# One core, a decoder layer: more expert tiles split ahead, gathers moved earlier, two score maps interleaved, gate loads reordered

## The chip, the core and the metric

The kernel runs on one NeuronCore of one Trainium2 chip. The metric is the device time of one execution in microseconds (us). Before the change the median of three runs is 1810.1 us (1809.93 to 1811.16). The engines are TensorE (PE for its matmuls, PEld for its weight loads), VectorE (DVE), ScalarE (ACT), GpSimd (POOL) and SyncE (SP, which only issues transfers). ACT and POOL also issue transfers, in their own order with their other work.

## The reference

One decoder layer on 512 tokens of width 1024, in two sub-layers, each `x <- LN_affine(ALPHA*x + gate*sublayer(h))` with `h = LN(x)*(1+scale)+shift`; shifts, scales and gates come from `silu(c) @ w_ada`.

Sub-layer 1 is a differential attention (8 heads, two score maps of 64 features per head, causal) beside a chunkwise matrix memory (4 heads), merged by sigmoid gates and projected. Sub-layer 2 is a retrieval over 128 x 128 = 16384 single-neuron experts:

```
q = (ht @ w_q).reshape(T, 8, 2, 64)            # 8 heads, two half keys
s = einsum('thpd,pnd->thpn', q, sub_keys)      # 2 maps of 128 scores per head
sv, si = top_k(s, 16)                          # of each map
cv, ci = top_k(sv0[:, None] + sv1[None], 16)   # of the 256 sums
g = softmax(cv);  eidx = i1 * 128 + i2
act = gelu(einsum('cd,chkd->chk', h, u_tab[eidx]))
out = einsum('chk,chkd->cd', g * act, v_tab[eidx])
```

Each token so uses 8 x 16 = 128 rows of `u_tab` and of `v_tab`.

## The kernel before

**Number format.** Every product of two f32 operands is three f16 matmuls (high x high, high x low, low x high). A weight tile of 128x1024 is loaded as f32 (`raw`, three buffers), split by ACT (the high part) and DVE (the low part) into `w2` (eight buffers), and used by PE. `presplit(n)` (L186) does the same ahead of time for tiles that are needed later: SP loads the tile into one of two halves of a buffer named `pre`, ACT and DVE split it, and ACT's queue writes both parts (512 KB) to `us` in DRAM. `load_p` (L199) then loads them with one transfer and no splitting; a tile that isn't in `us` goes through `raw`. `NP` tiles are pre-split: the 8 `q` tiles of layer two, then the `u` tiles in order.

**Layer one.** PE's program is written by hand (class `Ordered`): each matmul is chained to the one before it. Blocks of work that PE can do at any time (projections) stand in a queue `F`, and `F.run(ns)` puts so many nanoseconds of them between the steps of the attention. A step (`at_s`, L446) makes two score maps of one head and 128 queries: for each map three matmuls with 64 contraction rows (map 0 uses rows 0 to 63, map 1 rows 64 to 127), and one full-height matmul that adds the causal mask. DVE takes each map's row maximum, ACT the exponentials, DVE joins the maps. There are 32 steps; one `presplit(1)` stands in each of the first 27. In the merge that follows, eight rounds `j` each queue up to four blocks of 24 matmuls, and `presplit(PRE_M)` with `PRE_M` = 2 stands at the end of each round before `F.drain()`; one more follows the loop.

**Layer two, routing.** Token tile 0 (128 tokens) is served sparsely: `dots` gathers 128 rows of `u_tab` per token by 128 indirect transfers (POOL issues, 512 KB each) and DVE multiplies each with `h` and adds it up (L873); later 128 gathers of `v_tab` rows follow, with a multiply-add each (`accg`, L1235). Token tiles 1 to 3 are served densely: all 128 `u` tiles against 384 tokens, a gate mask multiplied in, and all 128 `v` tiles. `route(t)` (L940) finds the experts of tile t: `scores` (L925) makes one map of four heads, 12 matmuls of 64 rows and 128 columns, into one PSUM bank that ACT copies out to `sb`; DVE finds the top 16 of each of 16 maps and then of 8 sums; tiles 1 to 3 then build one-hot matrices on DVE and multiply them on PE to gate masks that go to DRAM (`gd`). `F` now holds the first 72 `u` tiles, whose results go to DRAM (`actd`). `some(dotg, 1)` lets DVE do one gather dot: after each of the four groups of maps and in each of the nine one-hot rounds, 13 per tile, 39 in all. Their gathers have two buffers there.

**Layer two, dense part.** The 32 rounds of `order` each take four `u` and `v` tiles. For 14 rounds the `u` products are made on the spot (`u_round`, 96 matmuls of 384 columns); for the last 18 they are loaded back from `actd` ("held" rounds). `gate(n)` multiplies the mask `gblk`, loaded by `gate_load`. `v_round` does 72 matmuls of 512 columns into six PSUM banks. The rest of the sparse work (89 dots, 128 multiply-adds) is let in by credits: 1.8 per `u` tile from the second `u_round` on, 1 per `v` tile, and what is left in the last round. `finish` normalises a token tile. The stage begins with a load of `h2r` (tile 0's `h`) from DRAM, `gate_row(gt2, g2r)` (eight transposes on PE, two copies on ACT) and six mask loads, ahead of the first `u_round`.

**What sets the order.** A scheduler orders each engine's program by the data dependencies and by where things stand in the code; on the chip each engine and each queue works its list in order, and waits at the first entry that isn't ready.

## Time and profile before

| | before |
|---|---|
| median of 3 runs | 1810.1 us |
| the profiled execution: time / span | 1810.87 / 1808.8 us |
| PE, DVE, ACT, POOL busy | 94%, 79%, 45%, 25% of the span |
| mean granted TensorE clock | 0.982 of full speed |
| DMA | 484.89 MB, mean 268 GB/s |

The span runs from the first to the last instruction; the execution's own time is 2.1 us longer. Reading in order of time: to 92 us start-up and first projections, 92 to 345 the attention steps, to 420 the matrix memory, to 572 the merge, to 640 the output projection and the start of layer two, 640 to 1036 the routing of tiles 0 to 3, 1036 to 1465 the dense rounds with `u` work, to 1795 the held rounds and the last one, then the end on DVE. A busy share is an average: a PE that shows 10 of 10 in a window has no idle time there, and there its own work sets the pace.

### The profile page before, as it was taken

How to read it: one execution, taken by the hardware profiler on the slowest of the kernel's cores; microseconds unless marked ns; L12 is line 12 of the kernel's file. 1: busy time of each engine (PE TensorE's matmuls, PEld its weight loads, DVE VectorE, ACT ScalarE, POOL GpSimd, SP SyncE). 2: the span in 40 equal slices, each digit the busy share in tenths (PEclk: the TensorE clock that was granted, in tenths of full speed). 3: DMA queues.
4: the chain of work that ended last, by engine and by line, in shares of the span. 5: the costliest groups of instructions: out<-in, count | busy, mean ns of one | idle time of the engine just before them, and what ended most of it. 6: DMA issues, size and time to landing. Idle time of an engine off the chain costs nothing.

```text
span 1808.8 us, 26501 instructions
## 1 busy us (share of the span) xinstructions
PE 1704.3 (94%) x9937; PEld 915.9 (51%) x9937; DVE 1423.5 (79%) x2702; ACT 813.1 (45%) x1279; POOL 452.6 (25%) x296
## 2 busy tenths in 40 slices
PE   5999999989999989999998899999999998988996
PEld 2444455445444666766655555555555543433443
DVE  7787877697666798969989658888878777577796
ACT  4556666564343433636737543333333333232332
POOL 0000000000000100110210135554556445345551
PEclk9999999989999999999999999999999999999999
DMA  8554754347776536895976999999999999988982
GB/s 337 170 191 168 248 195 142 105 157 273 273 277 231 210 114 222 285 306 193 305 258 222 334 347 357 389 349 343 341 376 331 333 336 321 342 287 320 331 325 80
DMA packets 223104, 484.89 MB, mean 268 GB/s; under 512 B 16000, under 2 KB 114560, under 8 KB 222976
## 3 DMA queue, kind: packets, MB, share of 16 engines
q1 hardware_dynamic: 124912, 286.06, 46.0%
q0 software_dynamic: 36864, 134.23, 20.2%
q10 hardware_dynamic: 61200, 62.92, 10.1%
q8 instruction: 77, 1.26, 0.3%
q14 instruction: 51, 0.42, 0.1%
HBM read 418.14 MB, written 65.01 MB: 267 GB/s over the span
## 4 chain that ended last, share of the span: by engine, by line
PE 58%; DVE 16%; DMA 9%; issue 8%; POOL 4%; ACT 3%; ACTq 1%; SPq 0%; DVEq 0%; POOLq 0%
PE mm L101 32%; PE s L101 15%; PE tr L101 6%; POOL gat L865 3%; PE o L101 3%; DVE w L169 2%; DMA gat<-in_v_dram,ev 2%; DMA gd<-gstage 1%; PE tr L104 1%; DMA vraw<-in_v_dram 1%; DMA raw<-in_u_dram 1%; DVE accg L1235 1%; DVE gat L873 1%; ACTq L914 1%; DMA at<-actd 1%
## 5 line engine op out<-in xcount | busy, mean ns | idle before, releaser
L101 PEld LDWEIGHTS <-w 128*128 128x128 f16 x7176 | 690.5, 99 | 669.3 <-issue 30.1
L101 PE MATMUL mm<-h2T,w 128*128 128x384 f16 (+2 forms) x3288 | 558.0, 327 | 12.0 <-ACT ast L857 7.4
L101 PE MATMUL s<-w,w 128*128 128x512 f16 x1152 | 275.4, 384 | 25.7 <-DVE w L169 25.7
L865 POOL DMA_INDIRECT gat<-in_v_dram,ev x128 | 240.3, 1878 | 227.6 <-DVE accg L1235 210.9
L865 POOL DMA_INDIRECT gat<-in_urows_dram,eu x128 | 179.5, 1403 | 447.6 <-DVE gat L873 352.0
L169 DVE SCALAR_TENSOR_TENSOR w<-raw,w 128x1024 f16<-128x1024 f32 x180 | 218.8, 1219 | 73.6 <-ACT w L168 73.1
L168 ACT ACTIVATE w<-vraw 128x1024 f16<-128x1024 f32 x128 | 134.9, 1055 | 284.2 <-DMA vraw<-in_v_dram 158.4
L168 ACT ACTIVATE w<-raw 128x1024 f16<-128x1024 f32 x180 | 188.2, 1053 | 85.6 <-DMA raw<-in_u_dram 34.1
L101 PE MATMUL mm<-h1T,w 128*128 128x512 f16 x960 | 219.0, 379 | 1.8 <-DVE cva L624 1.8
L101 PE MATMUL tr<-w,w 128*128 128x512 f16 x768 | 187.0, 380 | 0.0
L169 DVE SCALAR_TENSOR_TENSOR w<-vraw,w 128x1024 f16<-128x1024 f32 x128 | 155.2, 1217 | 20.2 <-ACT w L168 20.0
L1235 DVE SCALAR_TENSOR_TENSOR accg<-gat,wg,accg 128x1024 f32<-128x1024 f32 x127 | 162.3, 1278 | 10.1 <-DMA gat<-in_v_dram,ev 9.5
L1283 DVE TENSOR_TENSOR at<-at,gblk 128x1536 f32<-128x1536 f32 x32 | 56.2, 1755 | 81.1 <-DMA at<-actd 70.7
L873 DVE SCALAR_TENSOR_TENSOR gat<-gat,rows 128x1024 f32<-128x1024 f32 x89 | 107.9, 1220 | 12.5 <-DMA gat<-in_urows_dram,eu 12.4
L101 PE MATMUL mm<-w,h1T 128*128 128x512 f16 x456 | 107.7, 382 | 3.6 <-ACT h1T L168 1.8
L101 PE MATMUL o<-w,w 128*128 128x512 f16 x384 | 105.4, 385 | 0.0
L101 PEld LDWEIGHTS <-h1T 128*128 128x128 f16 x672 | 58.3, 98 | 66.0 <-issue 2.5
L165 POOL TENSOR_TENSOR ss<-ss,mhalf 128x4 f32<-128x4 f32 x8 | 8.1, 1017 | 314.7 <-DVE ss L510 284.2
L857 ACT ACTIVATE at<-mm 128x384 f32<-128x384 f32 x56 | 27.4, 489 | 129.8 <-PE mm L101 126.3
L1050 ACT ACTIVATE gstage<-tr 128x512 f32<-128x512 f32 x96 | 56.5, 598 | 55.3 <-PE tr L101 37.9
L169 DVE SCALAR_TENSOR_TENSOR pre<-pre 128x1024 f16<-128x1024 f32 x44 | 53.8, 1222 | 31.4 <-ACT pre L168 30.6
L101 PEld LDWEIGHTS <-onehot 128*128 128x128 f16 x768 | 64.0, 148 | 19.6 <-issue 9.5
(460 smaller groups left out, 1837.0 us busy)
## 6 DMA issues: line engine op xcount, KB each, us to landing
vraw<-in_v_dram SPq DMA_DIRECT2D x128, 512.0 KB, 7.5
raw<-in_u_dram SPq DMA_DIRECT2D x92, 512.0 KB, 6.5
raw<-in_wz_dram SPq DMA_DIRECT2D x64, 512.0 KB, 4.3
w<-us SPq DMA_DIRECT2D x52, 512.0 KB, 4.5
wad<-in_w_ada_dram SPq DMA_DIRECT2D x48, 512.0 KB, 5.1
gd<-gstage ACTq DMA_DIRECT2D x24, 1024.0 KB, 9.3
gblk<-gd SPq DMA_DIRECT2D x64, 384.0 KB, 9.9
us<-pre ACTq DMA_DIRECT2D x44, 512.0 KB, 4.1
```

Source lines behind the costliest of these rows:

```text
L101: self._link(self.tc.nc.tensor.matmul(*a, **k))
L104: self._link(self.tc.nc.tensor.transpose(*a, **k))
L165: G.tensor_tensor(o, i, mhalf[:, :i.shape[1]], op=ALU.pow)
L168: A.activation(hi, src, AF.Copy, scale=scale)
L169: V.scalar_tensor_tensor(lo, src, scale, hi, op0=ALU.mult, op1=ALU.subtract)
L857: A.activation(dst, ps[:, :TD], AF.Gelu, scale=RU)
L865: P.before(G.indirect_dma_start(out=g_, out_offset=None, in_=table, in_offset=bass.IndirectOffsetOnAxis(ap=e[:, k:k + 1], axis=0)))
L873: V.scalar_tensor_tensor(g_, g_, 1.0, ring["h2r"], op0=ALU.mult, op1=ALU.mult, accum_out=wg[:, k:k + 1])
L914: nc.scalar.dma_start(actd[k], a.rearrange("p a b -> p (a b)"))
L1050: A.activation(st[:, :, 4 * q4:4 * q4 + 4], ps.rearrange("p t i -> p i t"), AF.Copy, scale=1.0 / S_G)
L1235: V.scalar_tensor_tensor(accg, g_, wg[:, k:k + 1], accg, op0=ALU.mult, op1=ALU.add)
L1283: V.tensor_tensor(av, av, GB[q_ // 2][:, :, e].rearrange("p g e t -> p e g t"), op=ALU.mult)
```

## The change

- `NP` 44 to 64: `u` tiles 36 to 55 are pre-split too. 13 of them stand in the attention steps (a second `presplit` in every other one of the first 27 steps, after the transposes), so 40 there; the merge has 3 instead of 2 per round, 24 in all, each now followed by `F.run(5500)` rather than together; none is left after the loop.
- `some(dotg, 1)` stands after every second map search and every second search in the sums: 8 + 4 + 9 = 21 per tile, 63 in all. 65 dots are left for the dense part.
- `at_s` and `scores` make both maps in turn: a matmul of map 0, the same of map 1, and so on; in `at_s` both masks follow, then both maxima. `scores(t, hq)` fills two PSUM banks; for tiles 2 and 3 both are made at the end of the routing of the tile before, where one was.
- `gate_row(gt2)` and a 512 KB store of its result go to the start of layer two; the dense part loads `h2r` and `g2r` together (1 MB) from DRAM. The first four mask loads and this load come after the first `u_round`'s loads in the code, two more after them.

The core of the diff:

```
-NP = 44
+NP = 64
+PRE_H = 0.5
-PRE_M = 2
+PRE_M = 3
+FILL_P = 5500
...
-                for m in range(2):
-                    r = slice(64 * m, 64 * m + 64)
-                    sm = ps_s()
-                    sms.append(sm)
-                    P.matmul(sm[:, :n], q[r, 0, qs], k[r, 0, :n], start=True, stop=False)
-                    P.matmul(sm[:, :n], q[r, 0, qs], k[r, 1, :n], start=False, stop=False)
-                    P.matmul(sm[:, :n], q[r, 1, qs], k[r, 0, :n], start=False, stop=False)
+                sms = [ps_s(), ps_s()]
+                for a, b in ((0, 0), (0, 1), (1, 0)):
+                    for m in range(2):
+                        r = slice(64 * m, 64 * m + 64)
+                        P.matmul(sms[m][:, :n], q[r, a, qs], k[r, b, :n],
+                                 start=a + b == 0, stop=False)
+                for sm in sms:
                     P.matmul(sm[:, qs], identb, negm, start=False, stop=True)
+                for m, sm in enumerate(sms):
                     V.tensor_reduce(nm[:, m:m + 1], sm[:, :n], axis=AX.X, op=ALU.max, negate=True)
...
+                if n < PRE_N:
+                    presplit(int((n + 1) * PRE_H) - int(n * PRE_H))
...
-                presplit(PRE_M)
+                for _ in range(PRE_M):
+                    presplit(1)
+                    F.run(FILL_P)
                 F.drain()
...
-                    if n < 3:
-                        scores(t, *banks[n + 1])
+                    if n == 1:
+                        scores(t, 1)
...
-                    if t > 0:
-                        some(dotg, DOT_S)
+                        if t > 0 and k % 2 == 1:
+                            some(dotg, DOT_S)
...
+                    if t > 0 and h % 2 == 1:
+                        some(dotg, DOT_S)
...
-        nc.sync.dma_start(h2r, h2d)
-        gate_row(gt2, g2r)
...
+                    if n == 0 and i == 3:
+                        for k in range(4):
+                            gate_load(0, k)
+                        nc.sync.dma_start(rows[:, 0:2], h2d)
...
-            for k in range(6):
-                gate_load(k // 4 * 2, k % 4)
             u_round(0, SP_0)
+            for k in range(2):
+                gate_load(2, k)
```

PE's program in an attention step, before, from the third matmul of map 0 on (`s_803` and `s_809` are the PSUM banks of the two maps, `identb` the weights of the mask matmul):

```order
L101 LDWEIGHTS q_624
L101 MATMUL s_803<-k_657,q_624 128x128
L101 LDWEIGHTS identb_82
L101 MATMUL s_803<-negm_88,identb_82 128x128
L101 LDWEIGHTS q_624
L101 MATMUL s_809<-k_657,q_624 128x128
L101 LDWEIGHTS q_624
L101 MATMUL s_809<-k_657,q_624 128x128
```

The same step after; `s_803` and `s_804` are the two maps:

```order
L103 LDWEIGHTS q_624
L103 MATMUL s_803<-k_657,q_624 128x128
L103 LDWEIGHTS q_624
L103 MATMUL s_804<-k_657,q_624 128x128
L103 LDWEIGHTS identb_82
L103 MATMUL s_803<-negm_88,identb_82 128x128
L103 LDWEIGHTS identb_82
L103 MATMUL s_804<-negm_88,identb_82 128x128
```

Map 0's mask stood between the maps; now the six narrow matmuls alternate and both masks stand behind them. The number of instructions is the same.

SP's queue at the start of the dense part, before (`raw` are `u` tiles, `gblk` mask loads, the first row of `h2d` the load of `h2r`):

```order
L173 DMA raw<-in_u_dram 128x1024 x37
L1187 DMA rows_10955<-h2d 128x1024
L173 DMA raw<-in_u_dram 128x1024 x2
L1259 DMA gblk<-gd 128x6x128 x3
L173 DMA raw<-in_u_dram 128x1024 x2
L1259 DMA gblk<-gd 128x6x128 x3
L173 DMA raw<-in_u_dram 128x1024 x2
L1259 DMA gblk<-gd 128x6x128
```

The same place after:

```order
L175 DMA raw<-in_u_dram 128x1024 x23
L1312 DMA vraw<-in_v_dram 128x1024
L1272 DMA gblk<-gd 128x6x128 x4
L1293 DMA rows_11039<-h2d 128x2048
L1272 DMA gblk<-gd 128x6x128 x3
L1312 DMA vraw<-in_v_dram 128x1024
```

The `u` tiles up to the tenth of the dense part now stand ahead of every mask load, and the load from `h2d`, twice as large, behind four of them.

DVE's program at the end, before (`accg` is the sparse tile, `fo` a dense one, `w` the last splits ahead of it):

```order
L1235 SCALAR_TENSOR_TENSOR accg<-gat,wg,accg 128x1024 x4
L1330 SCALAR_TENSOR_TENSOR fo<-s,rows_10955 128x512
L1235 SCALAR_TENSOR_TENSOR accg<-gat,wg,accg 128x1024
L1202 TENSOR_TENSOR fo<-fo,ax_5393 128x512
L1238 TENSOR_TENSOR accg<-accg,rows_10955 128x512 x2
L1202 TENSOR_TENSOR accg<-accg,ax_5393 128x512 x2
L1330 SCALAR_TENSOR_TENSOR fo<-s,rows_10955 128x512 x2
L1214 TENSOR_SCALAR m_16304<-m_16304 128x1
L1202 TENSOR_TENSOR fo<-fo,ax_5393 128x512 x2
L1212 TENSOR_SCALAR m_16304<-m_16304 128x1
L1219 SCALAR_TENSOR_TENSOR accg<-accg,m_16304,rows_10955 128x512 x2
L1221 SCALAR_TENSOR_TENSOR accg<-accg,m_16304,rows_10955 128x512 x2
```

The same place after:

```order
L171 SCALAR_TENSOR_TENSOR w<-at,w 128x1536
L171 SCALAR_TENSOR_TENSOR w_16332<-vraw,w_16332 128x1024
L1347 SCALAR_TENSOR_TENSOR fo<-s,rows_11039 128x512
L1215 TENSOR_TENSOR fo<-fo,ax_5473 128x512
L1347 SCALAR_TENSOR_TENSOR fo<-s,rows_11039 128x512
L1215 TENSOR_TENSOR fo<-fo,ax_5473 128x512
L1227 TENSOR_SCALAR m_16365<-m_16365 128x1
L1347 SCALAR_TENSOR_TENSOR fo<-s,rows_11039 128x512
L1215 TENSOR_TENSOR fo<-fo,ax_5473 128x512
L1225 TENSOR_SCALAR m_16365<-m_16365 128x1
```

The last multiply-adds of `accg` and its normalisation stood among those of the first dense tile; after the change they stand seven rounds earlier, between the `v` splits, and none is left here.

## Rows read from the trace of the kernel before

**Rows 1.** Stages: stretch, then busy PE, PEld, DVE, ACT, POOL; clock, DMA, GB/s.
```profile
92.00:290.00 198.00, 192.04 (x1113) 96.25 (x1112) 156.10 (x341) 126.16 (x290) 5.12 (x5) 1.00 0.58 204
...
420.00:572.00 152.00, 152.00 (x713) 69.80 (x712) 97.93 (x133) 61.45 (x70) 2.46 (x1) 1.00 0.80 287
...
675.00:790.00 115.00, 113.59 (x884) 76.38 (x884) 96.00 (x319) 53.88 (x76) 15.12 (x14) 1.00 0.84 272
790.00:916.00 126.00, 122.10 (x934) 80.51 (x935) 112.03 (x307) 70.90 (x96) 16.62 (x13) 1.00 0.81 264
916.00:1036.00 120.00, 108.05 (x799) 71.78 (x799) 110.06 (x277) 71.09 (x94) 14.76 (x11) 0.96 0.79 257
...
1060.00:1465.00 405.00, 405.00 (x2186) 213.75 (x2185) 339.42 (x370) 151.57 (x179) 221.95 (x147) 1.00 0.97 352
1465.00:1705.00 240.00, 214.26 (x953) 94.31 (x952) 167.09 (x132) 75.33 (x67) 112.51 (x53) 0.96 0.90 322
```

**Rows 2.** Timeline of PE, an attention step: start, length (us), instruction, [idle before].
```profile
256.72 0.82 PE L101 MATMUL s<-k,q 64*128 64x512 f16 x3
257.47 0.23 PE L101 MATMUL s<-negm,identb 128*128 128x128 bf16 x1
257.63 0.82 PE L101 MATMUL s<-k,q 64*128 64x512 f16 x3
...
258.45 2.75 PE L101 MATMUL mm<-h1T,w 128*128 128x512 f16 x12
```

**Rows 3.** Timeline of PE, one bank of routing scores and its successor.
```profile
626.11 0.84 PE L101 MATMUL s<-kT,qT 64*128 64x128 f16 x12
626.88 0.66 PE L104 MATMUL tr<-ident,n 128*128 128x128 f32 x4
```

**Rows 4.** Score matmuls alone, 50 ns stretches: stretch, PE busy (matmuls in flight).
```profile
619.45:619.50 0.05, 0.05 (x4) 0.00 (x0) 0.00 (x0) 1.00 1.05 328
...
619.85:619.90 0.05, 0.05 (x8) 0.00 (x0) 0.00 (x0) 1.00 0.40 164
```

**Rows 5.** Waits of DVE from 92 to 290: total us, times, longest.
```profile
DVE pre L169 <- ACT pre L168: 15.2, 8, 3.5
DVE cc L472 <- ACT pm L468: 8.9, 9, 1.4
...
DVE ss L512 <- POOL ss L165: 5.6, 5, 1.2
```

**Rows 6.** Groups by line: busy us, mean ns of one, idle before.
```profile
L169 DVE SCALAR_TENSOR_TENSOR pre<-pre 128x1024 f16<-128x1024 f32 x44 | 53.8, 1222 | 31.4 <-ACT pre L168 30.6 <-DMA pre<-in_u_dram 0.5
L873 DVE SCALAR_TENSOR_TENSOR gat<-gat,h2rr 128x1024 f32<-128x1024 f32 x39 | 47.3, 1214 | 4.8 <-DMA gat<-in_urows_dram,eu 4.8
```

**Rows 7.** Waits of DVE from 640 to 1040: total us, times, longest.
```profile
DVE sv L917 <- ACT sb L934: 18.2, 4, 7.8
```

**Rows 8.** Timeline of PE in the routing of tile 3, its longest stall.
```profile
954.88 10.33 PE L101 MATMUL mm<-h2T,w 128*128 128x384 f16 x46 [5.17 <-ACT ast L857]
```

**Rows 9.** Timeline of PE where the dense part begins.
```profile
1035.53 0.65 PE L101 MATMUL mm<-h2T,w 128*128 128x384 f16 x3
...
1040.90 1.12 PE L104 MATMUL tr<-ident,mcgt 128*128 128x128 f32 x4 [4.28 <-ACT gstage L1050]
1041.80 17.84 PE L101 MATMUL mm<-h2T,w 128*128 128x384 f16 x96
```

**Rows 10.** Waits of PE from 1460 to 1760: total us, times, longest.
```profile
PE s L101 <- DVE w L169: 25.7, 7, 5.4
```

**Rows 11.** Timeline of PE, the last of these seven waits.
```profile
1700.25 2.40 PE L101 MATMUL s<-w,w 128*128 128x512 f16 x7 [3.68 <-DVE w L169]
```

**Rows 12.** Timeline of DVE at the end.
```profile
1784.41 1.28 DVE L1238 TENSOR_TENSOR accg<-accg,rows 128x512 f32<-128x512 f32 x2
...
1796.08 1.28 DVE L1330 SCALAR_TENSOR_TENSOR fo<-tr,rows 128x512 f32<-128x512 f32 x2
...
1804.40 1.41 DVE L1221 SCALAR_TENSOR_TENSOR fo<-fo,rs,rows 128x512 f32<-128x512 f32 x2
```

More of the change, by code (lines that the diff above doesn't have):

```diff
@@ L923, in body, with scores @@
             SB = {}
[L925 removed]
+            def scores(t, hq):
                 ts = slice(t * 128, (t + 1) * 128)
[L927 to L928 removed]
+                pss = [ps_s(), ps_s()]
                 for k in range(4):
                     h = 4 * hq + k
[L931 to L936 removed]
+                    for a, b in ((0, 0), (0, 1), (1, 0)):
+                        for p in range(2):
+                            r = slice(64 * p, 64 * p + 64)
+                            P.matmul(pss[p][:, k * 128:(k + 1) * 128], qT[r, h, a, ts], kT[r, b],
+                                     start=a + b == 0, stop=a == 1)
+                for p, ps in enumerate(pss):
+                    sb = t2("sb", (128, 4, 128))
+                    A.activation(sb, ps.rearrange("p (a b) -> p a b", a=4), AF.Copy,
+                                 scale=1.0 / (S_ACT * S_ACT))
+                    SB[t, hq, p] = sb
             banks = [(hq, p) for hq in range(2) for p in range(2)]
@@ L1005, in route @@
                 if 0 < t and t + 1 < NT:
-                    scores(t + 1, 0, 0)
+                    scores(t + 1, 0)
                 if t == 0:
@@ L1161, in body @@
             V.tensor_add(h2r, h2r, shr)
-            nc.scalar.dma_start(h2d, h2r)
+            nc.scalar.dma_start(h2d[:, 0], h2r)
+            g2s = t4("g2s")
+            gate_row(gt2, g2s)
+            nc.scalar.dma_start(h2d[:, 1], g2s)
             F.add("h2", weave(h2_part(1, 3), out3, H2_1))
@@ L1185, in body @@
         rows = big([128, 4, 1024], F32, "rows2")
-        g2r, lg, lb, h2r = [rows[:, k] for k in range(4)]
-        nc.sync.dma_start(h2r, h2d)
-        gate_row(gt2, g2r)
+        h2r, g2r, lg, lb = [rows[:, k] for k in range(4)]
         with pool(name="vp", bufs=1) as vp:
@@ L1284, in gate @@
                                 op=ALU.mult)
-                w = vp.tile([128, 2, 4, TD], F16, name="w", tag="w", bufs=2)
-                split(w[:, 0], w[:, 1], at, S_WT)
-                WT[n] = w
+                if n not in WT:
+                    WT[n] = vp.tile([128, 2, 4, TD], F16, name="w", tag="w", bufs=2)
+                split(WT[n][:, 0], WT[n][:, 1], at, S_WT)
             ACC = [[ps_s(), ps_s()], [ps_s(), ps_o()],
```

17 lines of the change are left out of this document (4 added, 13 removed).

## The prediction

> **What bounds the kernel now.** I read the profile in this order: busy time and clock by stage, PE's waits in each stage, then the timeline of PE and of DVE at the places that the change touches.
>
> The stages [rows 1] show who sets the pace. In the attention steps (92 to 290) PE is busy 192.0 of 198 us and DVE 156.1. In the merge (420 to 572) and in the dense rounds with `u` work (1060 to 1465) PE has no idle time at all, with DMA at 0.80 and 0.97. In the routing DVE fills up: 96 of 115 us for tile 1, 112 of 126 for tile 2, 110 of 120 for tile 3, where PE falls to 108. In the held rounds (1465 to 1705) PE is busy 214.3 of 240 with DMA at 0.90: PE is kept waiting there. So a cut of PE work pays where PE is full and nobody else is near it; DVE work moved forward costs where DVE has nothing to spare.
>
> Two unlike stalls: PE waits 4.28 us for the transposes of `gate_row` where the dense part begins [rows 9], and seven times, 25.7 us in all, for a split of `at` in the held rounds [rows 10].
>
> **The change part by part.** All against the profiled execution, 1810.87 us (span 1808.8 and 2.1 around it), 0.8 above the median.
>
> *Score maps in the attention.* At 512 columns a step goes from 256.72 to 258.45, 1.73 us [rows 2]. Three matmuls last 0.75 to the mask's start; 3 x 512 columns at 2.4 GHz are 0.64, so 0.11 goes with the change from half to full height. The mask takes 0.16 until the second map starts: 0.05 for its columns, again 0.11. Do two row halves run at once? Before, they meet only in the routing scores, and there the number of matmuls in flight rises from 4 to 8 around the seam of two banks [rows 4]: yes, as far as that shows. By the Trainium skill, page "TensorEngine Tiling (Array Packing)", section Key Properties, tiles of the array work independently, and a change of tiling mode drains the array; the trace agrees with the second by the 0.11 us twice. With both maps in turn a step saves 0.64 x n/512 for n columns plus some 0.2 for two fewer changes of height: 0.36, 0.52, 0.68 and 0.84 us for the four sizes, 0.60 on average, 32 steps 19.2; about 27 of them, 16.2, lie in 92 to 290.
>
> But DVE gets 13 more pre-splits there, 13 x 1.222 = 15.9 us [rows 6]: 156.1 + 15.9 = 172.0. Some of its waits lie inside the chain of a step and stay: 8.9 for the exponentials and 5.6 for POOL [rows 5], together 186.5. The 15.2 for ACT's half of the pre-splits may go (ACT is ahead when DVE is late) or stay: 186.5 to 201.7, beside PE's 198 - 16.2 = 181.8. So here the bound passes from PE to DVE; I take 192, half of those waits, a gain of 6. The page has a section that speaks against the change, PSUM Bottleneck: tiling speeds up TensorE but not the evacuation of PSUM, which may become the bottleneck. By it 16.2 would be gained on PE and only what DVE leaves be seen; the trace bears it out with DVE at 156 of 198. The five steps after 290 have no pre-splits and gain 5 x 0.6 = 3. **Attention: -9** (bounds -19.2, and 201.7 - 198 = +3.7 with nothing gained after 290).
>
> *Merge.* 17 pre-splits there become 24. Seven more move 7 x 1.05 MB in 152 us, 48 GB/s on top of 287 [rows 1]; the dense rounds carry 352 with PE full, so DMA can hide it. DVE has 54 us free for 8.6. A pre-split's load that waits on SP for its half of `pre` holds the weight loads behind it; spread singly, it finds its half free more often. **+1** (0 to +6: 7.3 MB at 352 GB/s are 21 us, a third of it uncovered when weight loads queue behind pre-splits).
>
> *`gate_row` moved.* Eight transposes and a store go to the start of layer two; four took 0.9 at the low clock [rows 9]. **+1** (0.5 to 1.8).
>
> *Routing scores.* A bank of 12 matmuls lasts from 626.11 to 626.88, 0.77 us [rows 3]; two in turn should last about that. Eight pairs: 6.2. Tile 0's overlap in part already, and tile 3 is paced by DVE. **-4** (-6.2 to -0.5).
>
> *Gather dots and missing splits in the routing.* 24 dots more at 1.214 and 0.08 for reading the sum [rows 6]: 31.1 us, 10.4 per tile. The splits of `u` 36 to 55 go: 20 x 1.22 = 24.4, nearly all within tile 2. So DVE has +10.4 in tile 1 (19 us idle [rows 1]), -14.0 in tile 2, +10.4 in tile 3, where only 10 us are idle. Of the 43 us idle in the three tiles DVE spends 18.2 waiting for `sb` at the tile borders [rows 7]; with both maps of the next tile made early those waits should go, and DVE's order after the change has 8 of tile 3's 16 searches among tile 2's one-hots instead of 4. ACT, waiting in its list for DVE, is what stops PE in tile 3 for 5.17 us [rows 8]; the dots lengthen just that chain. I take +3 for tile 1, -3 for tile 2 (PE idle 3.9), +2 for tile 3. **+2** (-5, most of PE's idle time in tiles 2 and 3 other than the 5.17 and the 3.9; to +12, tile 3's dots in full). Gathers: what is next late is the two-buffer ring, with dots every 4 us.
>
> *Start of the dense part.* PE ends the routing's `u` work at about 1036.0 and starts the next at 1041.8, and 96 x 384 columns, 15.4 us at 2.4 GHz, take 17.84 [rows 9], some at 1.2 GHz after the stall. Without `gate_row` both go: 5.8 + 2.4 = 8.2. In SP's queue ten `u` tiles stand before the first mask load, so the weights are there sooner; the masks are needed by PE only two `u` rounds later (31 us), though on DVE the first `gate` waits for them in its list with the splits of the next `u` tiles behind it. DMA is near its limit from here on (0.97), so I take **-5** (-8.2 to -1).
>
> *24 gathers fewer in the dense part.* Credits are unchanged: 13 x 11.2 = 145.6 items by round 12, then 4 per round. 217 items lasted to the last round; 193 end in round 24, (193 - 145.6)/4 = 11.9 rounds later. In the `u` rounds PE is full before and after: nothing. Of the seven waits in the held rounds only the last falls in the freed rounds, 3.68 us [rows 11], with 0.7 for matmuls at the low clock (7 in 2.40 us). **-4.5** (-10 if the wait before it goes too, -1 if the mask and `at` loads cause it alone).
>
> *The end.* `accg`'s last multiply-add and normalisation, five entries of about 1.3 us and 6.6 in all, stand among the dense tiles' work from 1784.41 on, and DVE is busy nearly without a break up to 1805.8 [rows 12]. They go seven rounds earlier. Then PE's last matmuls, ending near 1795, are waited for. **-4.5** (-6 to -2).
>
> Sum: -9 + 1 + 1 - 4 + 2 - 5 - 4.5 - 4.5 = -23: 1787.9 beside the profiled execution, 1787 beside the median.
>
> **Rivals.**
>
> *PE gets its whole gain in the attention*: DVE takes the pre-splits in its idle 42 us and in waits for PE that vanish. For it: PE's waits there are short and DVE's lists run steps ahead. Against: 172 us of work and fixed waits of 14.5. Attention -19 instead of -9: 1777.
>
> *The row halves don't overlap* when they alternate every matmul; only the changes of height are saved. For it: rows 4 is one seam. Attention 32 x 0.2 = 6.4 less the DVE load, -2 instead of -9; scores -0.5 instead of -4: 1797.5.
>
> *Slower: DVE is the path through both places where work was added.* In the attention its 15.9 come on top of 198 less the 7.5 that go when PE is earlier, +8; in tiles 1 and 3 the dots come on PE's path in full, +20.8, while tile 2 gains 3. Against -9 and +2 that is +17 and +16 more: 1820. It decides where DVE's idle time is all of the kind that stays. Against: 18.2 of the 43 us idle in the three tiles are waits for `sb` that the change makes early [rows 7].
>
> *What is gained is given back*: the dense part starts earlier but DMA at 0.97 holds it, and attention and routing cancel out. Then only the two last terms stay less 5 of contention: about 1806.
>
> **How the numbers follow.** Forecast 0.45 (its own range 1780 to 1794), whole gain 0.20, no overlap 0.20, given back 0.08, slower 0.07. About 0.2% (3.6 us) can be told from no change: faster 0.89, same 0.04 (half of given back), slower 0.07. The range for 8 in 10 reaches to both neighbours and the bounds of the dense terms beyond them: 1771 to 1805.
>
> **What would show it.** An attention step at 512 columns of about 0.9 us instead of 1.73 from first score to the next block (right), 1.5 (no overlap). DVE busy over 90% and PE's waits for DVE longer from 92 to 290. The merge with PE full as before. In tile 3 PE's stall at ACT near 5 us or, if the slower rival holds, 15. No gap at the first dense `u` tile. The last gather of `v` seven rounds before the end, none of the seven waits in those rounds, and DVE done within 9 us of PE's last matmul. Wrong: PE's idle time in 92 to 290 above 20 us, or a merge that shows waits for `raw`.

## The result, and the profile after

The changed kernel takes 1853.7 us (median of 4 runs, 1850.2 to 1862.2) beside 1810.0 for the kernel before on the same chip: a ratio of 1.025, 95% interval 1.0212 to 1.0287. It is slower by 44 us where 23 less were forecast, and outside the range. The profiled execution takes 1855.5 us, its span is 1853.4.

Five moments, the same in every trace, cut the span into six stretches: ACT's first and last split of `yT` (a merge round ends with each), the index `ev` on DVE at the end of routing tile 0, ACT's first eviction into `at` (dense part), and DVE's last split of `at`.

| stretch | before | after | change | forecast |
|---|---|---|---|---|
| start to first `yT` (attention) | 433.2 | 448.0 | +14.8 | -9 |
| first to last `yT` (merge) | 133.6 | 158.1 | +24.5 | +1 |
| last `yT` to `ev` | 106.1 | 109.8 | +3.7 | +1 |
| `ev` to first `at` (routing, start of dense) | 378.2 | 379.9 | +1.7 | -7 |
| first `at` to last split of `at` (dense) | 714.3 | 716.3 | +2.0 | -4.5 |
| to the end | 43.4 | 41.3 | -2.1 | -4.5 |

So 39 of the 44.6 us by which the span grew went in layer one, where the 20 pre-splits went. The stages of the changed kernel (columns as in [rows 1]; attention, merge, routing tiles 1 to 3, dense rounds, held rounds; its line numbers are 2 to 17 higher than before's):

```profile
92.00:309.00 217.00, 189.99 (x1116) 94.14 (x1115) 171.36 (x355) 139.25 (x306) 5.86 (x5) 0.94 0.72 249
437.00:611.00 174.00, 157.58 (x708) 71.06 (x707) 104.50 (x136) 67.10 (x76) 2.46 (x1) 0.94 0.82 294
716.00:1087.00 371.00, 346.00 (x2662) 228.79 (x2661) 323.55 (x935) 179.64 (x249) 73.85 (x63) 0.97 0.88 291
1106.00:1511.00 405.00, 403.90 (x2183) 213.34 (x2181) 335.63 (x343) 149.30 (x178) 229.97 (x144) 1.00 0.97 356
1511.00:1751.00 240.00, 215.51 (x959) 95.10 (x958) 168.59 (x133) 72.77 (x65) 102.78 (x50) 0.96 0.91 321
```

In the attention and the merge PE now stands idle for 27 and 16 us, and the granted clock is 0.94, yet no other engine is full: DVE is busy 171 of 217 and 105 of 174. Nobody is the bound; the engines wait for one another. The clock costs on top: of the attention's projection matmuls, 389 took 400 ns on average, where 392 took 379 before, so some 8 us more; part of the stretch ran at 1.2 instead of 2.4 GHz. What ACT waits for from 92 to 309 (total us, times, longest):

```profile
ACT pre L170 <- DMA us<-pre: 31.6, 14, 4.4
...
ACT pre L170 <- DMA pre<-in_u_dram: 4.3, 3, 3.3
...
ACT pre L170 <- DMA pre<-in_wq_dram: 3.3, 2, 2.7
```

The first row did not exist before. `pre` has two halves for loads and two for results, so a pre-split's first write waits until the result of two pre-splits earlier has landed in DRAM. How such a wait spreads shows in the timelines of ACT and then DVE at one place (start, length, instruction, idle before it and who ended it):

```profile
195.98 1.06 ACT L170 ACTIVATE w<-raw 128x1024 f16<-128x1024 f32 x1
199.86 1.06 ACT L170 ACTIVATE pre<-pre 128x1024 f16<-128x1024 f32 x1 [2.82 <-DMA us<-pre]
...
202.63 0.58 ACT L470 ACTIVATE pm<-s,nm 128x384 f32<-128x384 f32 x1 [1.72 <-DVE nm L467]
```
```profile
198.00 0.55 DVE L466 TENSOR_REDUCE nm<-s 128x1 f32<-128x384 f32 x1
200.95 1.22 DVE L171 SCALAR_TENSOR_TENSOR pre<-pre 128x1024 f16<-128x1024 f32 x1 [2.39 <-ACT pre L170]
202.09 0.16 DVE L467 TENSOR_SCALAR nm<-nm 128x2 f32<-128x2 f32 x1
```

Both maxima of an attention step are there at 198.55. The little scaling of `nm` stands behind a pre-split in DVE's list, the pre-split waits for ACT's half, ACT for a store: the exponentials start some 3.5 us later than DVE's two maxima alone would let them. The score banks come free later, and PE, which had other work until then, waits:

```profile
203.35 0.81 PE L103 MATMUL s<-k,q 64*128 64x512 f16 x5 [1.16 <-ACT pm L470]
```

Its two largest waits from 92 to 309; the first is for a bank of projections that DVE's convolution (`cva`) has not read yet, so an evicting engine that runs late is behind both:

```profile
PE mm L103 <- DVE cva L626: 9.6, 4, 2.8
PE s L103 <- ACT pm L470: 9.5, 8, 2.6
```

In the merge ACT's waits are mostly for loads, below.

Of the steps in the dense part, the stall at its start has only changed its owner. PE, then ACT (answers [rows 9]):

```profile
1083.83 8.45 PE L103 MATMUL mm<-h2T,w 128*128 128x384 f16 x51
1096.34 16.83 PE L103 MATMUL mm<-h2T,w 128*128 128x384 f16 x86 [4.06 <-ACT at L863]
```
```profile
1095.80 0.87 ACT L863 ACTIVATE at<-mm 128x384 f32<-128x384 f32 x2 [4.27 <-DMA actd<-ast]
```

The first eviction of the dense part now waits for the last store of the routing. ACT waited for that store before, too (3.4 us at 1051), but PE had started later, after the stall at `gate_row`, and did not stand still for it. The held rounds keep their seven waits of PE (answers [rows 10], total, times, longest):

```profile
PE s L103 <- DVE w L171: 24.5, 7, 5.6
```

And at the end PE finishes its 24 matmuls near 1841.6, with DVE's last entry 8 us behind (before, 11 behind 1795; answers [rows 12]):

```profile
1836.29 5.34 PE L103 MATMUL tr<-w,w 128*128 128x512 f16 x24
```
```profile
1848.56 1.41 DVE L1234 SCALAR_TENSOR_TENSOR fo<-fo,rs,rows 128x512 f32<-128x512 f32 x2
```

### The profile page after: what moved, and what is told of

It is laid out like the page before. It is cut to its first block, busy times and chain, and to the rows that moved or that the text cites. A ratio compares the mean times of both kernels' runs of the same rounds, so it can differ in the third digit from the quotient of the medians.

```text
span 1853.4 us, 26591 instructions
## 1 busy us (share of the span) xinstructions
PE 1700.3 (92%) x9937; PEld 908.7 (49%) x9937; DVE 1422.7 (77%) x2702; ACT 811.2 (44%) x1279; POOL 440.2 (24%) x296
## 3 DMA queue, kind: packets, MB, share of 16 engines
q10 hardware_dynamic: 64224, 73.93, 11.3%
## 4 chain that ended last, share of the span: by engine, by line
PE 32%; DVE 25%; DMA 22%; issue 9%; ACT 6%; POOL 5%; SPq 1%; ACTq 0%; DVEq 0%; POOLq 0%
PE mm L103 16%; PE s L103 8%; PE tr L103 5%; DVE w L171 4%; DMA us<-pre 4%; POOL gat L871 4%; DMA pre<-in_u_dram 4%; DMA vraw<-in_v_dram 3%; PE o L103 2%; DMA gat<-in_urows_dram,eu 2%; DVE gat L879 2%; DVE accg L1248 2%; DMA wad<-in_w_ada_dram 2%; DMA gat<-in_v_dram,ev 2%; DVE pre L171 1%
## 5 line engine op out<-in xcount | busy, mean ns | idle before, releaser
L103 PE MATMUL s<-w,w 128*128 128x512 f16 x1152 | 274.8, 384 | 24.5 <-DVE w L171 24.5
L871 POOL DMA_INDIRECT gat<-in_v_dram,ev x128 | 230.8, 1803 | 208.9 <-DVE accg L1248 194.5
L871 POOL DMA_INDIRECT gat<-in_urows_dram,eu x128 | 175.6, 1372 | 407.7 <-DVE gat L879 280.6
L103 PE MATMUL mm<-h1T,w 128*128 128x512 f16 x960 | 230.4, 393 | 15.6 <-DVE cva L626 9.6
L171 DVE SCALAR_TENSOR_TENSOR w<-raw,w 128x1024 f16<-128x1024 f32 x160 | 195.0, 1221 | 41.6 <-ACT w L170 41.1
L170 ACT ACTIVATE w<-vraw 128x1024 f16<-128x1024 f32 x128 | 132.3, 1051 | 216.1 <-DMA vraw<-in_v_dram 150.6
L170 ACT ACTIVATE w<-raw 128x1024 f16<-128x1024 f32 x160 | 167.6, 1052 | 111.8 <-DMA raw<-in_u_dram 87.0
L171 DVE SCALAR_TENSOR_TENSOR pre<-pre 128x1024 f16<-128x1024 f32 x64 | 78.3, 1223 | 72.5 <-ACT pre L170 72.2
L103 PE MATMUL mm<-w,h1T 128*128 128x512 f16 x456 | 109.4, 387 | 9.5 <-DVE q L171 5.4
L170 ACT ACTIVATE pre<-pre 128x1024 f16<-128x1024 f32 x64 | 67.6, 1056 | 107.4 <-DMA pre<-in_u_dram 59.4
L879 DVE SCALAR_TENSOR_TENSOR gat<-gat,rows 128x1024 f32<-128x1024 f32 x65 | 79.1, 1222 | 22.7 <-DMA gat<-in_urows_dram,eu 22.6
L879 DVE SCALAR_TENSOR_TENSOR gat<-gat,h2rr 128x1024 f32<-128x1024 f32 x63 | 76.7, 1219 | 20.3 <-DMA gat<-in_urows_dram,eu 20.2
(461 smaller groups left out, 1797.9 us busy)
```

Of the source, the lines that this page charges most:

```text
L103: self._link(self.tc.nc.tensor.matmul(*a, **k))
L170: A.activation(hi, src, AF.Copy, scale=scale)
L171: V.scalar_tensor_tensor(lo, src, scale, hi, op0=ALU.mult, op1=ALU.subtract)
L871: P.before(G.indirect_dma_start(out=g_, out_offset=None, in_=table, in_offset=bass.IndirectOffsetOnAxis(ap=e[:, k:k + 1], axis=0)))
L879: V.scalar_tensor_tensor(g_, g_, 1.0, ring["h2r"], op0=ALU.mult, op1=ALU.mult, accum_out=wg[:, k:k + 1])
```

## The experiments

All by the moments of the table above, each from one profiled execution; two kernels with the same layer one (`a` and `i` below) have their first `yT` at 433.6 and 428.8, so a difference of 5 us between two single traces is nothing. With 40 pre-splits it may be more: `s`, which differs from the changed kernel only by two buffers fewer for q and k, has it 11 us earlier, and the changed kernel's own four executions lie 12 us apart. "Attention" is the number of pre-splits there, "merge" likewise.

| run | attention, merge | first `yT` | merge us | `ev` to `at` | `at` to last split | median or single time |
|---|---|---|---|---|---|---|
| before | 27, 17 | 433.2 | 133.6 | 378.2 | 714.3 | 1810 |
| after | 40, 24 | 448.0 | 158.1 | 379.9 | 716.3 | 1853.7 |
| a old pre-splits | 27, 17 | 433.6 | 133.7 | 404.1 | 715.6 | 1836.9 |
| b only pre-splits | 40, 24 | 446.8 | 159.2 | 373.2 | 713.5 | 1840.2 |
| c attention 13 | 40, 17 | 449.3 | 133.7 | 369.9 | 711.9 | 1817.1 |
| d merge 7 | 27, 24 | 432.4 | 159.1 | 375.4 | 714.9 | 1835.3 |
| e loads ahead | 40, 24 | 445.4 | 157.6 | 373.8 | 712.8 | 1841.3 |
| f raw ring | 40, 24 | 549.3 | 246.2 | 376.7 | 711.3 | 2046.4 |
| g before, 13 | 13, 17 | 429.8 | 133.6 | 384.5 | 711.9 | 1815.0 |
| h in turn, 13 | 13, 17 | 413.0 | 133.6 | 412.9 | 717.1 | 1829.4 |
| i no dots | 27, 17 | 428.8 | 133.7 | 367.1 | 718.1 | 1802.3 |
| j spare loads | 27, 17 | 437.8 | 140.9 | 378.5 | 711.7 | 1823.8 |
| k half `w_ada` | 27, 24 | 433.7 | 153.9 | 376.8 | 714.6 | 1831.3 |
| l short low half | 40, 24 | 433.9 | 155.6 | 387.1 | 714.4 | 1844.6 |
| n deep merge | 27, 24 | 431.6 | 142.4 | 376.9 | 716.6 | 1823.9 |
| o burst of three | 27, 24 | 435.8 | 145.8 | 376.4 | 711.2 | 1822.0 |
| p in turn, 13, no dots | 13, 17 | 413.4 | 133.7 | 377.0 | 719.7 | 1792.0 |
| q fewer dots | 13, 17 | 412.7 | 133.6 | 367.2 | 734.6 | 1797.9 |
| r three results | 40, 24 | 436.3 | 157.9 | 385.9 | 715.6 | 1849.7 |
| s eight `qk` | 40, 24 | 437.0 | 159.7 | 384.6 | 715.1 | 1849.6 |

### Which part, where: a, b, c, d

`a` is the changed kernel with the pre-splits put back; `b`, `c` and `d` are the kernel before with all 20, the attention's 13, the merge's 7:

```diff
 # a, on the changed kernel
-NP = 64
+NP = 44
-PRE_M = 3
+PRE_M = 2
-    if n < PRE_N:
-        presplit(int((n + 1) * PRE_H) - int(n * PRE_H))
-    for _ in range(PRE_M):
-        presplit(1)
-        F.run(FILL_P)
+    presplit(PRE_M)
 # b, on the kernel before: the opposite; c: of b the presplit under PRE_N alone, with NP = 57;
 # d: of b the loop alone, with NP = 51
```

a: 

> The changed kernel with its pre-splits put back as before (44 instead of 64, 27 of them in the attention, two at the end of each merge round); score maps in turn, 24 more dots, gate loads and gate_row as changed. Theory W (the 20 extra pre-splits cost it all: ACT, working in order, waits for a load or for the store of two pre-splits before): the merge ends about 40 us plus the PE gain of the attention earlier, 20 splits return to routing tile 2, so 1798 to 1812 us. Rival M (the alternating row halves, the dots or the moved loads lose a good part of the 44 us): 1825 us or more.

b: 

> The kernel before with only the 20 extra pre-splits (13 more in the attention, 7 more in the merge, spread as in the change). Theory W: the attention loses 16 to 26 us, the merge 24, routing tile 2 gets back 5 to 14: 1838 to 1855 us. Rival M: at most 1822 us.

c: 

> The kernel before with only the 13 extra pre-splits in the attention. Theory W: the store of the pre-split two before is waited for in the attention as in the changed kernel (29 us of ACT waits there), attention 12 to 20 us longer, merge unchanged, a little back in the routing: 1818 to 1828 us, and the merge as long as before (133.6 us from the first to the last yT). Rival M: within 6 us of before.

d: 

> The kernel before with only the 7 extra pre-splits in the merge, spread singly. Theory W: attention as before, merge 20 to 28 us longer (158 us instead of 133.6 between first and last yT), 2 to 6 back in the routing: 1826 to 1834 us. A rival D (the merge's loss is inherited: its weights come late because the attention ran late): merge within 5 us of before, 1808 to 1815.

Ratios to before: `a` 1.0154 (1.0137 to 1.0171), `b` 1.0171 (1.0152 to 1.0189), `c` 1.0050 (1.0033 to 1.0066), `d` 1.0149 (1.0133 to 1.0166). The stretches add up: the attention's 13 cost 14 to 16 there, the merge's 7 cost 25.5 there whether the attention ran late or not, which ends rival D. `b` came as theory W had it, `c` and `d` within 1.5 us of its ranges. But `a` fell out of theory W's range and lands at rival M's: its layer one is that of before, and between `ev` and the first `at` it loses 26. So something else in the change costs as much again, and the 20 splits that left the routing paid part of it in the changed kernel.

### The routing: i, and dots against dense part: q

```diff
 # i, on a: per searched bank one dot, as before; none among the pair searches
-        if t > 0 and k % 2 == 1:
-            some(dotg, DOT_S)
+    if t > 0:
+        some(dotg, DOT_S)
-    if t > 0 and h % 2 == 1:
-        some(dotg, DOT_S)
 # q, on p below
-DOT_S = 1
+DOT_S = 0
-SP_U = 2.8
+SP_U = 3.0
```

i: 

> The changed kernel with 44 pre-splits as before and the gather dots spread as before (39 in the routing, not 63); left of the change are the score maps in turn, the gate loads and gate_row. Theory Q (in the routing DVE is full, so 24 more dots cost their 1.21 us each): from ev to the first at of the dense part 382 us or less instead of 404.1, 1803 to 1814 us in all. Rival G (the moved gate loads or the scores in turn lose it): 395 us or more, 1825 or more.

q: 

> The run above with 27 dots in the routing instead of 39; the 12 others go to the dense part's u rounds, whose rate of gathers rises by 0.2 per u tile. Theory Q (DVE is full in the routing): 10 to 14 us earlier at the start of the dense part; dense part within 4 us: 1777 to 1789 us. Rival X (the 12 gathers of 0.52 MB come on top of a DMA at 0.97 in the dense part, 18 us at 353 GB/s): no faster than the run above.

`i` takes 0.9955 of before (0.9936 to 0.9974), 1802.3 us, a little under what theory Q expected. Its routing and the start of the dense part are 37 us shorter than with the dots, 1.5 us for each of 24 (`h` against `p` gives the same, 35.9), more than the 1.21 of a dot on DVE. Part of the difference is DVE's wait for the gathers themselves, which have two buffers: 17.4 us in 12 waits in `a`, 6.5 in one in `i`. The stretch from `ev` to the last eviction of the routing, `a` then `i` (columns as above):

```profile
677.00:1071.00 394.00, 350.26 (x2645) 229.28 (x2643) 345.53 (x954) 198.00 (x269) 75.97 (x63) 0.96 0.83 273
```
```profile
672.00:1030.00 358.00, 342.48 (x2661) 227.58 (x2659) 317.82 (x907) 197.82 (x267) 49.97 (x39) 0.99 0.81 266
```

PE's costliest wait in it, again `a` then `i`:

```profile
PE mm L103 <- ACT ast L859: 27.3, 6, 8.4
```
```profile
PE mm L103 <- ACT ast L859: 5.3, 2, 3.7
```

DVE is busy for about 88% in both; every dot on it makes the stretch longer, and PE waits in the place named in [rows 8], for ACT standing behind DVE. What `i` keeps of the change (scores in turn, `gate_row` and gate loads moved) is worth 378.2 - 367.1 = 11 us here, where the forecast had 9. `q` goes on in that direction: 12 dots fewer, the stretch 9.8 shorter. But the 12 gathers then stand in the dense part, which gets 14.9 longer: 0.9928 of before (0.9906 to 0.9950), beside 0.9896 (0.9869 to 0.9923) for `p`. That is rival X: no faster. Twelve dots cost no less in the dense part than in the routing, so their number before was about right.

### What a pre-split costs in the attention: g, h, l, f, r, s

```diff
 # g, on before; h, on a
-NP = 44
+NP = 30
-PRE_A = 1.0
+PRE_A = 0.5
 # l, on the changed kernel
-split(w[:, 0:1024], w[:, 1024:2048], raw, tables[kind][1])
+A.activation(w[:, 0:1024], raw, AF.Copy, scale=tables[kind][1])
+V.tensor_copy(w[:, 1024:2048], w[:, 0:1024])
 # f, on b
-raw, w = b[:, k % 2], b[:, 2 + k % 2].bitcast(F16)
+raw = wts.tile([128, 1024], F32, name="praw", tag="raw", bufs=3)
+w = b[:, k % 4].bitcast(F16)
 # r, on the changed kernel (pex[0]: a third buffer); s: the last two lines alone
-raw, w = b[:, k % 2], b[:, 2 + k % 2].bitcast(F16)
+raw, w = b[:, k % 2], (b[:, 2], b[:, 3], pex[0])[k % 3].bitcast(F16)
-tag="qk", bufs=10
+tag="qk", bufs=8
```

g: 

> The kernel before with 13 instead of 27 pre-splits in the attention (30 instead of 44 in all, the missing 14 splits come back in routing tile 1 and 2). Read is the time of the first yT, 433.2 before. Theory B (in the kernel before PE and the chain over DVE and ACT pace the attention about alike, so a cut of one of them alone moves nothing): 429 to 434. Rival V (DVE and the pre-splits alone pace it): 425 or earlier.

h: 

> The changed kernel with 13 pre-splits in the attention and 17 in the merge, score maps in turn. Read is the time of the first yT, 433.6 with 27 pre-splits there. Theory B: with both PE and DVE relieved the attention gets shorter, first yT at 425 or earlier. Rival S (the three score banks, two of which are now taken at the start of a step, keep a step waiting for the exponentials of the last one): 430 to 435, and PE's waits for the exponentials at the scores stay near 10 us.

l: 

> The changed kernel, where DVE's part of each pre-split is a plain copy of the high half (the low half of those weights is left out), which spares DVE part of its 1.22 us. Read is the first yT, 448.0 in the changed kernel. Theory V (DVE's time for the pre-splits sets the pace of the attention): earlier by about 40 times what the copy is shorter, 437 or earlier if it halves. Rival W (ACT's waits for the buffers of the pre-splits): 444 or later. The merge stays above 152 us by theory D.

f: 

> The kernel before with only the 20 extra pre-splits, whose loads use the ring of three weight buffers and whose results take turns in four slots of pre instead of two. Theory W: waits for the store of two pre-splits before vanish (from about 29 us to under 5 in the attention), and the first yT comes at 437 us or earlier instead of 446.8. Rival V (the 13 splits' own time on DVE is what the attention pays): first yT at 443 or later. In the merge the loads now share three buffers with the weights; no theory says which way that goes. 1820 to 1845 us.

r: 

> The changed kernel with a third buffer for the results of the pre-splits; its space comes from the ring of q, k and PT buffers, 8 instead of 10. Read are the first yT (448.0 in the changed kernel) and ACT's waits for stores of pre-splits from 92 to 309 us (31.6 there). Theory W: the waits for stores fall under 10 us and the first yT comes at 440 or earlier. Rival V (what the pre-splits cost there is their own time on DVE and ACT): waits for stores fall, first yT stays at 444 or later.

s: 

> The changed kernel with 8 instead of 10 buffers for q, k and PT and nothing else: what the space for the third buffer of the run above costs by itself. First yT between 446 and 454 us by either theory; the run above is read against this one.

`g` and `h` settle what the score maps in turn are worth. Of before, `a` and `h` from 92 to 290, the scores on PE (busy us, mean ns, idle before):

```profile
L101 PE MATMUL s<-k,q 64*128 64x384 f16 (+3 forms) x156 | 30.7, 303 | 2.2 <-ACT pm L468 2.2
```
```profile
L103 PE MATMUL s<-k,q 64*128 64x384 f16 (+3 forms) x156 | 17.0, 306 | 10.0 <-ACT pm L470 10.0
```
```profile
L103 PE MATMUL s<-k,q 64*128 64x384 f16 (+3 forms) x174 | 16.9, 300 | 0.0
```

The same matmuls keep PE 13.7 us less, so the row halves do run at once. With 13 pre-splits the first `yT` comes 16.8 earlier for it (413.0 against 429.8), with 27 it comes 0 to 4.4 earlier. With 40 the traces don't settle it: 445.4 to 449.3 without the maps in turn (`b`, `c`, `e`), with them 448.0 in the changed kernel, 436.3 and 437.0 in `r` and `s`. In `a` most of the 18 us saved on PE (13.7 here, 4.4 in the mask) is back: 7.8 as more waiting for the exponentials, 3.6 as more waiting for `cva`, some 5 as slower matmuls (means of 384 and 396 ns in its two groups of projections, 379 before; the granted clock was 0.97 from 142 to 290). That is theory B: at 27 pre-splits PE and the chain over ACT and DVE were level already, [rows 1] showed a full PE and hid the other. Taking 14 pre-splits away alone (`g`) gives 3.4 us, which is within the noise; with the maps in turn it gives 16 to 21.

From 13 to 40 pre-splits the attention with maps in turn grows by 35 us by the changed kernel's trace, by 24 by that of `s`. In `l` a pre-split takes 0.42 us of DVE instead of 1.22, and the first `yT` is 14 earlier than in the changed kernel, theory V's direction at under half its size (31 us of DVE work went); beside `s` it is only 3 earlier. So how much of the growth is DVE's time is not shown. What ACT's waits for stores add did not come apart either. `f` says nothing of it: its waits for stores are gone, but loads and weights share three buffers, PE waits for weight splits, and the first `yT` comes 102 us after that of `b`, the merge takes 87 more. `r` alone came out as theory W had it (436.3, no wait for stores among the longest), but its control `s` came at 437.0, so removing those waits gained nothing. The waits of ACT from 92 to 309 in `r`, then `s`:

```profile
ACT pre L170 <- DMA pre<-in_u_dram: 26.6, 12, 5.0
...
ACT pre L170 <- DMA pre<-in_wq_dram: 7.9, 4, 3.5
```
```profile
ACT pre L170 <- DMA us<-pre: 29.1, 12, 5.3
...
ACT pre L170 <- DMA pre<-in_u_dram: 4.0, 3, 2.8
```

One wait took the place of the other: with the results' buffers deeper, the two load buffers hold ACT for the same time: SP waits 34.9 us, 11 times, for DVE's half of an earlier pre-split before it can issue such a load, in `s` 34.7. Three result buffers and two load buffers are still a chain of two. `s` itself was expected at 446 or later and came at 437.0: fewer buffers for q and k did no harm. Why it is 11 us before the one trace of the changed kernel stays open.

### What a pre-split costs in the merge: e, j, k, n, o

```diff
 # e, on b, in the merge: behind each pre-split's store the load of the next
+    k >= 40 and preload(k + 1, end)
 # j, on before, in each merge round
+for half in range(4):
+    spare = fr.tile([128, 2, T], F16, name="spare", tag="qk", bufs=10)
+    P.before(nc.sync.dma_start(..., u[100 + j][:, (half % 2) * 512:(half % 2 + 1) * 512]))
 # k, on d, in the merge (n = 512; the product over it runs twice)
-nc.sync.dma_start(w, w_ada[8 * k + j])
+nc.sync.dma_start(w[:, 0:n], w_ada[8 * k + j][:, 0:n])
 # n, on d, in the merge: loads into pre[:, k % 4], results in two of the ten qk tiles
+for q in range(3):
+    preload(k + q)
+hi, lo = [deep[0]().rearrange("p a b -> p (a b)") for _ in range(2)]
 # o, on d
-for _ in range(PRE_M):
-    presplit(1)
-    F.run(FILL_P)
+presplit(PRE_M)
```

e: 

> The kernel before with only the 20 extra pre-splits, and in the merge the load of each pre-split issued one pre-split earlier, ahead of the w_ada loads of its round instead of behind them; the two halves of pre stay two. Theory W (ACT, in order, waits for a load that SP issues late): ACT's waits for pre loads in the merge fall from 50 us to under 15, the merge from 159 us between first and last yT to at most 148 (7 rounds of 14 transfers of 0.52 MB at the 352 GB/s of the dense rounds are 146), 1826 to 1832 us. Rival D (the traffic itself is too much): 155 us or more, 1837 to 1843.

j: 

> The kernel before, with four more loads of 0.26 MB in each merge round, into buffers that nothing reads: the bytes of the one pre-split more per round (load and store), without its work. Read is the time from the first to the last yT, 133.6 before, 159 with 7 pre-splits more. Theory D (the DMA has nothing left in the merge, every byte more takes its time): 152 us or more. Rival W (ACT, in order, waits for loads and stores of the pre-splits): 142 or less.

k: 

> The kernel before with 7 pre-splits more in the merge, where the four w_ada loads of a round bring half of their columns (used twice, so the modulation of layer one's gates is left wrong): the bytes per round are as before, with all pre-split work kept. Read is the time from the first to the last yT, 159.1 with whole loads. Theory D: 142 us or less. Rival W: 152 or more.

n: 

> The kernel before with 7 pre-splits more in the merge as in the change, but with four buffers for their loads, which are issued two pre-splits ahead, and ten half-size buffers for their results (free space of the attention's q and k). Read is the time from the first to the last yT, 133.6 before, 159.1 with two buffers each. Theory W (waiting for the buffers): 145 us or less, about the 141 that the bytes alone cost, and ACT's waits for pre loads and us stores under 15 us of 67. Rival C (the pre-splits' own work in the lists of ACT and DVE, wherever their data is): 152 or more.

o: 

> The kernel before with 7 pre-splits more in the merge, three in a row at the start of each round as the two were before, instead of spread singly. Theory W: the third in a row must wait for the first one's buffer, so the merge is no shorter than spread, 155 to 165 us. Rival P (what costs is that the pre-splits stand among the weight splits of a round): 146 or less.

Two rows of windows, `j` and `k` from their first to their last `yT`:

```profile
437.80:578.70 140.90, 137.27 (x637) 61.95 (x634) 86.87 (x118) 53.06 (x63) 2.46 (x1) 1.00 0.88 324
```
```profile
433.70:587.60 153.90, 138.40 (x639) 62.18 (x636) 96.89 (x157) 61.22 (x69) 2.46 (x1) 0.98 0.78 277
```

The same bytes per round without the pre-splits cost 7 us, at 324 GB/s; the pre-splits with the bytes per round of before cost 20, at 277. Rival D falls: the merge is not short of DMA, it is slow to ask for it. With twice the load buffers, loads two ahead and ten half-size result buffers (`n`) the 7 pre-splits cost 8.8 instead of 25.5, little more than their bytes. So buffers decide, theory W, though ACT's waits for loads are still 28.2 us (50.0 in `d`, and 13.8 for stores) where under 15 was expected; whether it is the load or the result buffers was not taken apart. Issuing the load earlier into the same two halves (`e`) gives only 1.6, which is where rival D was expected and theory W was not; ACT's waits for loads fall only to 41.6 us. So it is not SP's order alone.

`o` went against theory W and came as rival P had it: three in a row cost 12.2, half of what three spread singly cost. Spreading is half the loss. ACT's waits for stores do rise, as theory W said (26.8 us, 13.8 in `d`), but those for loads fall more (14.2, 50.0 in `d`). `d` shows why, in SP's queue, ACT and PE of one round:

```profile
488.94 6.97 SPq L312 DMA_DIRECT2D wad<-in_w_ada_dram  x3
495.95 0.43 SPq L196 DMA_DIRECT2D pre<-in_u_dram  x1
...
499.98 0.33 SPq L174 DMA_DIRECT2D raw<-in_wz_dram  x1
```
```profile
502.98 1.06 ACT L169 ACTIVATE pre<-pre 128x1024 f16<-128x1024 f32 x1 [5.25 <-DMA pre<-in_u_dram]
503.95 0.58 ACT L720 ACTIVATE gg<-mm 128x512 f32<-128x512 f32 x1
...
505.70 1.06 ACT L169 ACTIVATE w<-raw 128x1024 f16<-128x1024 f32 x1 [1.18 <-DMA raw<-in_wz_dram]
```
```profile
504.58 5.34 PE L102 MATMUL mm<-h1T,w 128*128 128x512 f16 x24 [1.10 <-ACT gg L720]
...
518.82 7.03 PE L102 MATMUL mm<-h1T,w 128*128 128x512 f16 x24 [3.72 <-ACT gg L720]
```

The load goes out at 495.95, behind `w_ada` loads that waited for their buffers, and lands 7.0 us later. ACT waits 5.25 for it; behind it stand the gate's tanh, which starts at 503.95 and frees PE's bank, and the next weight's split. The group after the longer stall takes 7.03 us instead of 5.34; the granted clock from first to last `yT` is 0.97, 1.00 before [rows 1]. All these waits for the tanh are 7.6 us, in 5 times. A larger piece stands at the end of the merge. PE has finished the last round's groups at 575.1, while ACT waits for the load of one more pre-split, with the round's last tanh, weight splits and `yT` behind it; PE can do 21 matmuls of the output projection and then waits. ACT, then PE:

```profile
586.41 1.06 ACT L169 ACTIVATE pre<-pre 128x1024 f16<-128x1024 f32 x1 [8.08 <-DMA pre<-in_u_dram]
```
```profile
592.20 1.69 PE L102 MATMUL mm<-w,yT 128*128 128x512 f16 x3 [11.96 <-ACT yT L169]
```

So of the 25.5 us, 11.3 are this stall up to the last `yT`, 7.6 the waits for the tanh, and in the rest PE is busy longer (140.3 instead of 133.6 us, for 639 matmuls instead of 621 and at the lower clock). The stall is 10.4 us in the changed kernel and 10.6 in `e`; it is 6 in `o`, 3 in `n`, 4.7 in `j`, and before there was none. In `o` two pre-splits follow each other right behind a round's `yT`, and only the third stands among the round's splits; a pre-split between the evictions and weight splits of a round makes those wait too.

### A version that beats both: p

```diff
 # p, on i
-NP = 44
+NP = 30
-PRE_A = 1.0
+PRE_A = 0.5
```

p: 

> The changed kernel with 39 dots in the routing as before and 13 pre-splits instead of 27 in the attention (30 in all, 44 before): score maps in turn, gate loads and gate_row as changed. Theory B: first yT near 413 us as in the run with 13 and the dots, some 16 to 20 earlier than with 27; the 14 splits cost 6 to 9 in the routing: 1788 to 1797 us. Rival: the splits in the routing cost their whole DVE time, 14 x 1.22 = 17 us: 1798 to 1803.

1792.0 us, 0.9896 of before (0.9869 to 0.9923): about 1% faster. What is left of the change in it: score maps in turn, gate loads and `gate_row`; the pre-splits of the attention are halved instead of raised, the dots are those of before. In its attention no wait of ACT for `pre` is left among the longest.

## Why the prediction was wrong

*Merge, +1 forecast, +24.5.* The step that failed: "DVE has 54 us free for 8.6. [...] spread singly, it finds its half free more often. +1". The busy times were right, and 7.3 MB more does fit, for 7 us (`j`). But free time of an engine says nothing of an entry that waits at the head of its list: in `d` ACT waits 50.0 us for loads of pre-splits and 13.8 for their stores, with PE's evictions and the last `yT` behind them. ACT, the one that waits, was not in this term at all, though [rows 6] had DVE's half of the pre-splits wait 30.6 us for it. And the spreading, counted as a help, cost half (`o` against `d`). The text named a merge with waits for `raw` as what would make it wrong; the waits were for `pre`.

*Attention, -9 forecast, +14.8.* "So here the bound passes from PE to DVE; I take 192" was right that PE stops being the bound and wrong on what takes over: DVE is busy 155 of 198 us from 92 to 290, 78%, where over 90% was to show it, and what took over is a chain of waits through ACT, DVE and the stores. (Half of [rows 5]'s 15.2 would also give 194, not 192.) By `a` the bound had passed before a single pre-split was added: the maps in turn alone gave between 0 and 4.4. The bound above, +3.7, took [rows 5]'s waits as fixed; with 40 pre-splits the waits for stores of two pre-splits before came new. `b`, `c` and `e`, without the maps in turn, show 13 pre-splits costing 12 to 16 there; in `s` and `r` the attention ends only 3 to 4 us later than before, so the size of this miss is less certain than that of the merge.

The sign given for a wrong forecast, PE idle for more than 20 us from 92 to 290, did come: 24.7. The gain on PE itself was sized well (19.2 for all steps; `h` against `g` shows 16.8), and a step at 512 columns lasts 0.88 us, where about 0.9 was forecast instead of 1.73 (the changed kernel; its next block starts at 103.48):

```profile
102.60 0.82 PE L103 MATMUL s<-k,q 64*128 64x512 f16 x6
103.36 0.28 PE L103 MATMUL s<-negm,identb 128*128 128x128 bf16 x2
```

The Trainium skill, page "TensorEngine Tiling (Array Packing)", section PSUM Bottleneck, warns that tiling speeds up TensorE and not what empties PSUM; these runs agree in so far as ACT and DVE read the score banks, with 16.8 us where ACT and DVE have 13 pre-splits to do and 0 to 4.4 where they have 27.

*Routing and the start of the dense part, -7 forecast, +1.7.* The scores and the start together are worth the 11 of `i` (9 forecast), although the first `at` still waits some 4 us for a store (4.1 in `i`). The term "dots and missing splits, +2" was mis-sized: the splits that leave give back 5 alone (`b`) and 24 beside the dots (`a` against the changed kernel), the 24 dots cost 1.5 us each while those splits are there (`a`, `i`), and in the changed kernel the two together come to 1.7 + 11 = 13, just past the upper bound of 12. "I take +3 for tile 1, -3 for tile 2, +2 for tile 3" let DVE's idle time of [rows 7] take most dots, which it did not; and the gathers' two buffers, named there as next late, did make DVE wait (20.2 us in the changed kernel, 4.8 before).

*Dense part, -4.5 and the end -4.5, measured +2.0 and -2.1.* `accg` was finished seven rounds early, as forecast, and the last of the seven waits came just before that instead of in the freed rounds. At the end PE's last matmuls are waited for, as forecast, but what DVE has to do behind them takes 8 us. The +3.7 after the last `yT` is not placed: `g`, `j` and `n`, without the moved `gate_row`, have it too (109.4, 109.5, 110.8).

*The rivals.* "Slower: DVE is the path through both places" had two of the three places and 0.07: +8 for the attention, where 14.8 came, +18 for the dots and splits, where 13 came. No rival had the merge, which is over half. "The row halves don't overlap" is refuted by the 17.0 us above. "Whole gain" would have needed the DVE side free, as `h` has it.

What stays open: how the 24 to 35 us that 27 pre-splits cost in the attention with maps in turn divide between DVE's time (3 to 14 by `l`), ACT's own 1.06 us each and its waits, since `r` exchanged one wait for another; and which of the buffers, for loads or for results, made `n` fast in the merge.

## What to carry to other kernels

When background work is put into the lists of in-order engines, count first its buffers: the round of load, split and store through two halves has a pace of its own, and when it is fed faster, whoever issues the next step holds everything behind it, however idle the engines look. A full engine is not the only bound if a second chain runs level with it: before cutting its work, find what happens to the other when the load changes; `g` and `h`, with less side work, show it. And side work can be cheaper in a row at a seam than spread between the steps that others wait for: in the merge here 12.2 us instead of 25.5.

## What the runs showed of the hardware that was not expected

The DMA carried 324 GB/s at a share of 0.88 in the merge with PE busy for 137 of 141 us (`j`); the 287 at 0.80 of [rows 1] was what was asked of it, not what it could give. Matmuls on the two row halves, alternating one by one, took 17.0 instead of 30.7 us for 156, so nearly half; the mask's row, 7.5 instead of 11.9 us for 52, fits the two changes of height that a step saves (0.17 us a step, where 0.2 was estimated).
